# First modulated input of a transformer kernel: built feature-major from a transposed x, its shift and scale as columns

## The chip, the cores and the metric

One core of one Trainium2 chip. The metric is the device time of one execution of the whole program in microseconds; lower is better. Engines are TensorE (PE), VectorE (DVE), ScalarE (ACT), GpSimd (POOL) and SyncE (SP, which here issues all DMAs). Times within the execution are counted from the start of the profiled span.

## What is computed

Two transformer layers (an attention mixer and a gated feed-forward each), then a third block, on a sequence of 256 tokens of 1024 features, in float32. The change touches only how the very first modulated input is made:

```python
shift, scale, gate = split((c @ mod_w[layer, 0] + mod_b[layer, 0])[:, None, :], 3)
h = rms_norm(x, norm_w[layer, 0, 0]) * (1.0 + scale) + shift
y = mixer_ab(h, ...)        # proj = h @ w_in: qa, k, v, gates, qb, kb, vb ...
```

with rms_norm(x, w) = x * rsqrt(mean(x * x) + 1e-6) * w. The vector c has 1024 features; shift and scale are each 1024 wide and the same for all tokens.

## The kernel before

**Products.** A float32 product is made from three products of rounded halves: every weight tile `raw` is split into `whi` (ScalarE, L256) and `wlo` (VectorE, L257), the input into `hhi` and `hlo`, and TensorE makes hhi·whi, hlo·whi and hhi·wlo (L178 to L180). h is held feature-major, as eight k-tiles of 128 features x 256 tokens.

**The start.** `start` makes h in two halves q of four k-tiles (512 features) each. `load(q, v, i)` brings the modulation weights (v = 0 scale, 1 shift) as half-megabyte DMAs and sums over the eight k-tiles kk of c: some kk go to TensorE as a 128x512 product with `cb`, c broadcast to 128 columns (L1550), the others to VectorE, which adds weight times c into `acc` (L1553). `total` adds acc by a product with ones (L1556). All 128 rows of the result are the same, so it stands along the free axis and fits x with tokens on the partitions: `scaled` makes norm weight times (1 + scale) as `ws` (L1566) and multiplies x by it (L1569), `shifted` multiplies by the root and adds the shift (L1575), transposes the eight 128x128 blocks with TensorE (L1578) and evacuates them as hhi (ScalarE, L187) and hlo (VectorE, L188).

**Behind it.** `q_halves` gives the projection qb in two halves of its contraction: `run(0, t)`, t = 0 to 3, uses k-tiles 0 to 3 of h (12 products each) and is called in `start`; `run(1, t)` uses k-tiles 4 to 7 and is called in `mixer_ab`, followed by kb (24 products), the token-major v (L830 to L832), the first scores (L658) and the first softmax (L669). Meanwhile VectorE adds the later modulations in the background (`macc`, L319), the first of them held back until the last hlo of the start.

**What sets the order.** TensorE runs in the order of the program. The order of the other engines' queues, SP's among them, is set by a scheduler when the program is built. Each queue is in order: an instruction that waits holds all behind it. SP's DMAs go round eight semaphores, so that a DMA is issued when the eighth before it has landed; weight tiles go round a ring of six `raw` buffers, splits round four `whi` and four `wlo`. The tiles of `start` share memory with those of the mixer, such as the bias tiles `T` (L844).

In the kernel after, lines up to the start are numbered five higher (L178 is 183, L257 is 262, L319 is 324).

## Time and profile before

| | us |
|---|---|
| median of 3 runs | 1219.04 (1218.2 to 1220.63) |
| the profiled execution | 1217.92 |
| its span | 1216.1 |
| PE busy | 1160.1 (95%) |
| DVE busy | 919.3 (76%) |
| ACT busy | 609.2 (50%) |
| POOL busy | 136.1 (11%) |

The profiled execution is 1.8 us longer than its span, and 1.1 us shorter than the median. Busy shares are averages over stages with different limits; the start, which the change touches, is the first 60 us.

### The profile page before, as it was taken

The numbers are of one execution on the slowest core, as the hardware profiler recorded it, in microseconds if no ns is written. First come the engines' busy times: TensorE is split into PE (matmuls) and PEld (weight loads), VectorE is DVE, ScalarE is ACT, GpSimd is POOL, SyncE is SP. The second block draws the span as 40 slices with busy tenths as digits, with TensorE's granted clock in tenths as the row PEclk, the third lists the DMA queues.
The fourth block names the chain that finished last, engine by engine and source line by source line (L and its number), as shares of the span: only waits on it lengthen the run. The fifth ranks groups of instructions, "written<-read, shape, count | busy, mean of one in ns | idle before, by whom it ended". The sixth has DMA issues, their size and how long they took to land.

```text
span 1216.1 us, 19237 instructions
## 1 busy us (share of the span) xinstructions
PE 1160.1 (95%) x7452; PEld 1010.3 (83%) x7452; DVE 919.3 (76%) x1352; ACT 609.2 (50%) x1107; POOL 136.1 (11%) x181
## 2 busy tenths in 40 slices
PE   6999999999998999999999799999999889999997
PEld 2786569999887965999988699998888657999985
DVE  5888668878759786997896898777569968666545
ACT  2466445444445655554468864544443324445433
POOL 2000010000001012200000200000028850000000
PEclk9999999999999999999999899999999889999999
DMA  9975768868865768777887488688454534665520
GB/s 353 415 263 191 260 242 303 316 219 322 330 221 205 298 217 349 284 293 266 324 314 290 162 299 314 227 300 350 173 195 152 191 139 173 243 234 189 203 103 34
DMA packets 49537, 302.66 MB, mean 249 GB/s; under 512 B 6155, under 2 KB 6283, under 8 KB 16934
## 3 DMA queue, kind: packets, MB, share of 16 engines
q1 hardware_dynamic: 49446, 301.44, 66.7%
q8 instruction: 58, 0.95, 0.3%
q14 instruction: 33, 0.27, 0.1%
HBM read 295.64 MB, written 5.78 MB: 248 GB/s over the span
## 4 chain that ended last, share of the span: by engine, by line
PE 63%; issue 18%; DVE 10%; POOL 3%; ACT 3%; DMA 3%; SPq 0%; POOLq 0%; DVEq 0%; ACTq 0%
PE ps L180 11%; PE ps L178 11%; PE ps L179 11%; PE y L518 5%; PE y L516 5%; PE y L517 5%; PE y L514 4%; PE tok L546 2%; DVE macc L319 2%; DVE wlo L257 1%; PE ps L1305 1%; PE ps L658 1%; DVE st L1357 1%; PE o L702 1%; PE ps L432 1%
## 5 line engine op out<-in xcount | busy, mean ns | idle before, releaser
L256 ACT ACTIVATE whi<-raw 128x1024 fp32r<-128x1024 f32 (+2 forms) x307 | 318.3, 1045 | 374.1 <-PE ps L179 145.6
L257 DVE TENSOR_TENSOR wlo<-raw,whi 128x1024 fp32r<-128x1024 f32 (+2 forms) x307 | 370.3, 1212 | 170.2 <-ACT whi L256 168.5
L180 PE MATMUL ps<-hhi,wlo 128*128 128x256 f32 x1488 | 421.5, 283 | 3.4 <-DVE wlo L257 3.4
L178 PE MATMUL ps<-hhi,whi 128*128 128x256 f32 x1488 | 423.3, 284 | 0.0
L179 PE MATMUL ps<-hlo,whi 128*128 128x256 f32 x1488 | 421.0, 283 | 0.0
L180 PEld LDWEIGHTS ps<-hhi,wlo 128*128 128x128 f32 x1488 | 285.4, 192 | 4.4 <-DVE wlo L257 4.4
L178 PEld LDWEIGHTS ps<-hhi,whi 128*128 128x128 f32 x1488 | 285.3, 192 | 2.3 <-issue 1.1
L179 PEld LDWEIGHTS ps<-hlo,whi 128*128 128x128 f32 x1488 | 285.4, 192 | 1.1 <-DVE wlo L257 0.2
L319 DVE SCALAR_TENSOR_TENSOR macc<-raw,c,macc 128x1024 f32<-128x1024 f32 x152 | 194.9, 1282 | 4.5 <-issue 2.2
L516 PE MATMUL y<-whi,gh 128*128 128x512 f32 x352 | 139.6, 397 | 0.0
L518 PE MATMUL y<-whi,gl 128*128 128x512 f32 x352 | 139.3, 396 | 0.0
L517 PE MATMUL y<-wlo,gh 128*128 128x512 f32 x352 | 139.0, 395 | 0.0
L309 POOL MEMSET macc<- 128x1024 f32 x19 | 18.8, 990 | 582.0 <-DVE mlo L334 556.5
L518 PEld LDWEIGHTS y<-whi,gl 128*128 128x128 f32 x352 | 66.6, 189 | 15.4
L517 PEld LDWEIGHTS y<-wlo,gh 128*128 128x128 f32 x352 | 66.6, 189 | 15.2
L516 PEld LDWEIGHTS y<-whi,gh 128*128 128x128 f32 x352 | 66.6, 189 | 14.9
L514 PE MATMUL y<-raw,o 128*128 128x512 f32 x128 | 57.3, 595 | 0.0
L617 DVE TENSOR_TENSOR g<-sg,ps 128x256 f32<-128x256 f32 x80 | 33.5, 418 | 29.7 <-PE ps L180 29.5
L399 POOL TENSOR_SCALAR ms<-ss 128x1 f32<-128x1 f32 x24 | 11.7, 486 | 377.9 <-ACT junk L409 374.0
L176 PE MATMUL ps<-h,raw 128*128 128x256 f32 x192 | 45.3, 392 | 5.0 <-DVE cvt L1435 5.0
L176 PEld LDWEIGHTS ps<-h,raw 128*128 128x128 f32 x192 | 37.2, 196 | 11.0 <-DVE cvt L1435 5.2
L514 PEld LDWEIGHTS y<-raw,o 128*128 128x128 f32 x128 | 23.5, 190 | 26.3 <-issue 25.1
(313 smaller groups left out, 1458.0 us busy)
## 6 DMA issues: line engine op xcount, KB each, us to landing
raw<-in_mod_dram SPq DMA_DIRECT2D x76, 1024.0 KB
raw<-in_ffn_g_dram SPq DMA_DIRECT2D x44, 1024.0 KB
raw<-in_ffn_u_dram SPq DMA_DIRECT2D x44, 1024.0 KB
raw<-in_ffn_d_dram SPq DMA_DIRECT2D x44, 1024.0 KB
raw<-in_ab_out_dram SPq DMA_DIRECT2D x8, 1024.0 KB
raw<-in_cd_out_dram SPq DMA_DIRECT2D x8, 1024.0 KB
raw<-in_s_c_dram SPq DMA_DIRECT2D x6, 1024.0 KB
raw<-in_s_out_dram SPq DMA_DIRECT2D x6, 1024.0 KB
```

What stands on the lines that cost most here:

```text
L176: mm(out, lh, rh, start=first, stop=last)
L178: mm(out, lh, rh, start=first, stop=False)
L179: mm(out, lh, rl, start=False, stop=False)
L180: mm(out, ll, rh, start=False, stop=last)
L256: self.nc.scalar.activation(hv, src, AF.Copy)
L257: self.nc.vector.tensor_tensor(lv, src, hv.bitcast(F32), ALU.subtract)
L319: nc.vector.scalar_tensor_tensor(acc, box["r"][:, kk % 2], c[:, kk:kk + 1], acc, ALU.mult, ALU.add)
L514: mm(ys[h][b], xh[:, k, c], wh[:, 0, sl], start=first, stop=last)
L516: mm(ys[h][b], xh[:, k, c], wh[:, 0, sl], start=first, stop=False)
L517: mm(ys[h][b], xh[:, k, c], wl[:, 0, sl], start=False, stop=False)
L518: mm(ys[h][b], xl[:, k, c], wh[:, 0, sl], start=False, stop=last)
L617: nc.vector.tensor_tensor(g, sg, pu, ALU.mult)
```

## The change

x comes transposed, as `xt` (eight tiles of 128 features x 256 tokens, 1 MB, in the old place of x in the DMA queue), and norm weight and the two biases as 24 columns `cols`. Scale and shift are wanted as columns, one number per feature on the partitions, so a 128x512 weight block is now the stationary operand, in four blocks of 128 columns, and one column of c is the moving one: four products of 128x1 (changed kernel, line 1554) instead of one of 128x512. `total` does the same with acc and a column of ones (line 1564), and a 128x4 instruction adds the bias and, for the scale, 1 (line 1567). The split of the eight kk between TensorE and VectorE becomes 1, 3, 5, 7 against 0, 2, 4, 6 for the first half and 3, 5, 7 against 0, 1, 2, 4, 6 for the second.

The mean of squares over features is a sum over partitions: ScalarE squares each tile of xt, TensorE adds it by sixteen products with a column of 1/1024 (line 1593). The root stands as a 128x2 tile with tokens on the partitions; the identity times it gives a diagonal, and ones times the diagonal (line 1603) spreads it over all partitions. VectorE multiplies xt by the norm weight and the spread root, in place (line 1605, eight times 128x256). `modulated` makes h from that with scale and shift as columns: t on VectorE (line 1574), hhi on ScalarE, hlo = t - hhi on VectorE (line 1576); nothing is transposed or evacuated. x itself, which the later residual wants, is loaded by a DMA of its own that the scheduler puts behind the last modulation load and ahead of qb's second half, kb and v.

```diff
@@ -128,6 +128,11 @@
     for x, k in enumerate(("ssm_c_re_2", "ssm_c_im_2")):
         ct[:, :, :, x] = I[k][0].reshape(16, 2, 16, 64).transpose(3, 0, 1, 2)[None]
     o["s5_b"], o["s5_cm"] = b.reshape(128, 1024), ct.reshape(128, 1024)
+
+    feat = lambda v: v.reshape(8, 128).T
+    o["xt"] = I["x"][0].T.reshape(8, 128, S).transpose(1, 0, 2)
+    b0 = I["mod_b"].reshape(12, D)
+    o["cols0"] = np.concatenate([feat(I["norm_w"][0, 0, 0]), feat(b0[1]), feat(b0[0])], 1)
     o["mod_bias"] = np.concatenate([I["mod_b"].reshape(12, D), I["b_mod_2"].reshape(9, D)])
     return o
 
@@ -1520,97 +1525,104 @@
         self.c2 = cp.tile([128, 8], F32, name="c2")
         self.x = cp.tile([128, 2, D], F32, name="x")
         with self.tc.tile_pool(name="start", bufs=1) as bp:
-            nw = bp.tile([1, D], F32, name="nw")
             ones = bp.tile([128, 128], F32, name="ones")
             nc.vector.memset(ones, 1.0)
-            cb = bp.tile([128, 8, 128], F32, name="cb")
-            nc.vector.tensor_copy(cb, self.c1.unsqueeze(2).to_broadcast([128, 8, 128]))
+            mean = bp.tile([128, 1], F32, name="mean")
+            nc.vector.memset(mean, 1.0 / D)
+            cols = bp.tile([128, 24], F32, name="cols")
+            xt = bp.tile([128, 8, 256], F32, name="xt")
             hh, hl = self.h = self.h_tiles()
-            rs = []
+            mm = nc.tensor.matmul
 
             def load(q, v, i):
+
 
                 if i == 0:
                     acc = bp.tile([128, 512], F32, name=f"acc{v}{q}")
-                    mods[v] = self.bank([512]), acc, True
+                    sums[v] = [self.bank([4]), acc, True]
                     nc.gpsimd.memset(acc, 0.0)
-                ps, acc = mods[v][:2]
+                ps, acc, _ = sums[v]
                 w = I["mod0"][q, v, i]
                 r = self.raw() if i == 0 and not (q and v) else bp.tile([128, 2048], F32, name="sraw", bufs=5)
                 r = r.rearrange("p (k n) -> p k n", k=4)
-                pairs = [r[:, 0:2], r[:, 2:4]]
                 for k in range(4):
                     kk = 4 * i + k
-                    r = pairs[k // 2][:, k % 2, :]
                     if k % 2 == 0:
-                        nc.sync.dma_start(out=pairs[k // 2], in_=w[:, k:k + 2])
-                        if kk == 0:
-                            nc.sync.dma_start(out=acc[0:1, :], in_=I["mod_bias"][1 - v:2 - v, 512 * q:512 * q + 512])
-                    if kk in (((1, 3, 5, 7), (1, 3, 5, 7)), ((3, 7), (3, 7)))[q][v]:
-                        nc.tensor.matmul(ps, cb[:, kk, :], r, start=mods[v][2], stop=False)
-                        mods[v] = ps, acc, False
+                        nc.sync.dma_start(out=r[:, k:k + 2], in_=w[:, k:k + 2])
+                    if kk in ((1, 3, 5, 7), (3, 5, 7))[q]:
+                        for b in range(4):
+                            mm(ps[:, b:b + 1], r[:, k, 128 * b:128 * b + 128], self.c1[:, kk:kk + 1],
+                               start=sums[v][2], stop=False, skip_group_check=True)
+                            sums[v][2] = False
                     else:
-                        nc.vector.scalar_tensor_tensor(acc, r, self.c1[:, kk:kk + 1], acc, ALU.mult, ALU.add)
-
-            def total(v):
-                nc.tensor.matmul(mods[v][0], ones, mods[v][1], start=False, stop=True)
-                return mods[v][0]
-
-            def scaled(q, ts):
-
-                sl = slice(512 * q, 512 * q + 512)
-                ws = bp.tile([128, 512], F32, name="ws0", bufs=1)
-                nb = self.bank([512])
-                nc.tensor.matmul(nb, ones[0:1, :], nw[:, sl], start=True, stop=True)
-                nc.scalar.activation(ws, nb, AF.Copy)
-                nc.vector.scalar_tensor_tensor(ws, total(0), 1.0, ws, ALU.add, ALU.mult)
-                for h in range(2):
-                    t = bp.tile([128, 512], F32, name="t0", bufs=4)
-                    nc.vector.tensor_tensor(t, self.x[:, h, sl], ws, ALU.mult)
-                    ts.append(t)
-
-            def shifted(q, ts):
-                sh = total(1)
-                for h, t in enumerate(ts):
-                    nc.vector.scalar_tensor_tensor(t, t, rs[h], sh, ALU.mult, ALU.add)
-                    pt = self.bank([4, 128])
-                    for j in range(4):
-                        nc.tensor.transpose(pt[:, j, :], t[:, 128 * j:128 * j + 128], self.ident)
-                    ks, cs = slice(4 * q, 4 * q + 4), slice(128 * h, 128 * h + 128)
-                    self.anchor = self.evac(hh[:, ks, cs], hl[:, ks, cs], pt)
-            mods, ta, tb = {}, [], []
+                        nc.vector.scalar_tensor_tensor(acc, r[:, k], self.c1[:, kk:kk + 1], acc, ALU.mult, ALU.add)
+
+            def total(q, v):
+
+                ps, acc, _ = sums[v]
+                for b in range(4):
+                    mm(ps[:, b:b + 1], acc[:, 128 * b:128 * b + 128], ones[:, 0:1], start=False, stop=b == 3,
+                       skip_group_check=True)
+                m = bp.tile([128, 4], F32, name=f"m{v}{q}")
+                nc.vector.scalar_tensor_tensor(m, ps, 1.0 - v, cols[:, 8 + 8 * v + 4 * q:12 + 8 * v + 4 * q], ALU.add, ALU.add)
+                return m
+
+            def modulated(q, ws, sh):
+                for b in range(4):
+                    k = 4 * q + b
+                    t = bp.tile([128, 256], F32, name="t0", bufs=3)
+                    nc.vector.tensor_scalar(t, xt[:, k], ws[:, b:b + 1], sh[:, b:b + 1], ALU.mult, ALU.add)
+                    nc.scalar.activation(hh[:, k], xt[:, k], AF.Identity, scale=ws[:, b:b + 1], bias=sh[:, b:b + 1])
+                    self.anchor = nc.vector.tensor_tensor(hl[:, k], t, hh[:, k].bitcast(F32), ALU.subtract).ins
+            sums = {}
             load(0, 0, 0)
+            nc.sync.dma_start(out=xt, in_=I["xt"])
             load(0, 0, 1)
-            nc.sync.dma_start(out=self.x, in_=I["x"][0].rearrange("(h p) d -> p h d", p=128))
-            nc.sync.dma_start(out=nw, in_=I["norm_w"][0, 0, 0:1])
-            self.neghalf = cp.tile([128, 4], F32, name="neghalf")
-            nc.vector.memset(self.neghalf, -0.5)
-            for h in range(2):
-                rs.append(self.rstd(*self.mean_sq([self.x[:, h, 512 * q:512 * q + 512] for q in range(2)], D)))
-            scaled(0, ta)
-            load(0, 1, 0)
+            nc.sync.dma_start(out=cols, in_=I["cols0"])
             self.c32 = cp.tile([128, C_W], F32, name="c32")
             nc.sync.dma_start(out=self.c32, in_=I["consts"])
             self.ident = self.c32[:, C_ID:C_ID + 128]
+            self.neghalf = cp.tile([128, 4], F32, name="neghalf")
+            nc.vector.memset(self.neghalf, -0.5)
+
+            ms = self.bank([2])
+            for k in range(8):
+                sq = bp.tile([128, 256], F32, name="sq", bufs=3)
+                nc.scalar.activation(sq, xt[:, k], AF.Square)
+                for h in range(2):
+                    mm(ms[:, h:h + 1], sq[:, 128 * h:128 * h + 128], mean, start=k == 0 and h == 0, stop=k == 7 and h == 1,
+                       skip_group_check=True)
+            ss = self.sp.tile([128, 2], F32, tag="ss", name="ss")
+            nc.vector.tensor_copy(ss, ms)
+            rs = self.rstd(ss)
+            load(0, 1, 0)
+            rb = self.bank([256])
+            for h in range(2):
+                dg = bp.tile([128, 128], F32, name="dg", bufs=2)
+                nc.vector.tensor_scalar(dg, self.ident, rs[:, h:h + 1], None, ALU.mult)
+                mm(rb[:, 128 * h:128 * h + 128], ones, dg, start=True, stop=True)
+            for k in range(8):
+                nc.vector.scalar_tensor_tensor(xt[:, k], xt[:, k], cols[:, k:k + 1], rb, ALU.mult, ALU.mult)
+            ws = total(0, 0)
             load(0, 1, 1)
             nc.sync.dma_start(out=self.c2, in_=I["cond_2"][0].rearrange("(p k) -> p k", p=128))
             nc.scalar.activation(self.c2, self.c2, AF.Silu)
-            shifted(0, ta)
+            modulated(0, ws, total(0, 1))
 
             self.early = prepare, run = self.q_halves(I["ab_qb"], hh, hl)
-            early = {}
             with self.tc.issue_after(self.anchor):
                 early = {t: prepare(0, t) for t in range(4)}
             load(1, 0, 0)
             load(1, 0, 1)
             run(0, 0, early[0])
             run(0, 1, early[1])
-            scaled(1, tb)
+            ws = total(1, 0)
             load(1, 1, 0)
             load(1, 1, 1)
             run(0, 2, early[2])
-            shifted(1, tb)
             run(0, 3, early[3])
+            modulated(1, ws, total(1, 1))
+            nc.sync.dma_start(out=self.x, in_=I["x"][0].rearrange("(h p) d -> p h d", p=128))
 
     def setup(self):
         nc, I, cp, ap = self.nc, self.I, self.cp, self.ap
```

What the scheduler made of it: VectorE's queue, from the spread root to the first splits of qb. acc_201 and acc_255 (before), acc_261 and acc_319 (after) are the second half's scale and shift sums; the hlo here are those of the first half. Before:

```order
L188 TENSOR_TENSOR hlo<-ps,hhi 128x4x128
L1553 SCALAR_TENSOR_TENSOR acc_201<-raw,c_80,acc_201 128x512
L188 TENSOR_TENSOR hlo<-ps,hhi 128x4x128
L257 TENSOR_TENSOR wlo<-raw,whi 128x512 x4
L1553 SCALAR_TENSOR_TENSOR acc_201<-sraw,c_80,acc_201 128x512
L1553 SCALAR_TENSOR_TENSOR acc_255<-sraw,c_80,acc_255 128x512
L1553 SCALAR_TENSOR_TENSOR acc_201<-sraw,c_80,acc_201 128x512
L1553 SCALAR_TENSOR_TENSOR acc_255<-sraw,c_80,acc_255 128x512
L1553 SCALAR_TENSOR_TENSOR acc_201<-sraw,c_80,acc_201 128x512
L1553 SCALAR_TENSOR_TENSOR acc_255<-sraw,c_80,acc_255 128x512 x4
```

After:

```order
L1558 SCALAR_TENSOR_TENSOR acc_319<-sraw,c_80,acc_319 128x512 x2
L1567 SCALAR_TENSOR_TENSOR m_225<-ps,cols 128x4
L1558 SCALAR_TENSOR_TENSOR acc_319<-sraw,c_80,acc_319 128x512
L1574 TENSOR_SCALAR t_227<-xt,m_204,m_225 128x256
L1574 TENSOR_SCALAR t_231<-xt,m_204,m_225 128x256
L1574 TENSOR_SCALAR t_235<-xt,m_204,m_225 128x256
L1558 SCALAR_TENSOR_TENSOR acc_319<-sraw,c_80,acc_319 128x512
L1576 TENSOR_TENSOR hlo<-t_227,hhi 128x256
L1576 TENSOR_TENSOR hlo<-t_231,hhi 128x256
L1576 TENSOR_TENSOR hlo<-t_235,hhi 128x256
L1574 TENSOR_SCALAR t_239<-xt,m_204,m_225 128x256
L1576 TENSOR_TENSOR hlo<-t_239,hhi 128x256
```

All five sums of the second half's shift (one stands two rows above this piece) are now ahead of the first half's first hlo, and the splits of qb follow right behind it; before, nine sums stood behind the hlo and the four splits of qb.

TensorE's queue between the first two and the last two first halves of qb. Before:

```order
L180 MATMUL ps<-hhi,wlo 128x256
L1564 MATMUL ps<-nw,ones 128x512
L1556 MATMUL ps<-acc_201,ones 128x512
L1550 MATMUL ps<-sraw,cb 128x512 x2
L178 MATMUL ps<-hhi,whi 128x256
```

After:

```order
L185 MATMUL ps<-hhi,wlo 128x256
L1564 MATMUL ps<-ones,acc_261 128x1 x4
L1554 MATMUL ps<-c_80,sraw 128x1 x12
L183 MATMUL ps<-hhi,whi 128x256
L184 MATMUL ps<-hlo,whi 128x256
```

The norm weight's product is gone; the total of the scale and the shift's products are four and twelve of one column, where one and two of 512 columns stood.

VectorE's queue around the last hlo and the splits for kb (128x1024) and v (128x816); macc are background sums. Before:

```order
L188 TENSOR_TENSOR hlo<-ps,hhi 128x4x128
L257 TENSOR_TENSOR wlo<-raw,whi 128x512
L257 TENSOR_TENSOR wlo<-raw,whi 128x1024
L257 TENSOR_TENSOR wlo<-raw,whi 128x816 x3
L319 SCALAR_TENSOR_TENSOR macc<-raw,c_80,macc 128x1024 x2
L257 TENSOR_TENSOR wlo<-raw,whi 128x816
```

After:

```order
L1576 TENSOR_TENSOR hlo<-t_389,hhi 128x256
L324 SCALAR_TENSOR_TENSOR macc<-raw,c_80,macc 128x1024
L1632 TENSOR_TENSOR iddup<-c_126 128x128
L324 SCALAR_TENSOR_TENSOR macc<-raw,c_80,macc 128x1024
L262 TENSOR_TENSOR wlo<-raw,whi 128x1024
L324 SCALAR_TENSOR_TENSOR macc<-raw,c_80,macc 128x1024
L262 TENSOR_TENSOR wlo<-raw,whi 128x816
```

Two background sums went ahead of kb's split and a third ahead of v's first.

## Rows read from the trace of the kernel before

**Rows 1.** Table by stage, columns by engine: busy (instructions); PEclk, DMA share, GB/s.

```profile
0.00:5.00 5.00, 0.00 (x0) 0.00 (x0) 1.14 (x4) 1.28 (x1) 3.54 (x9) 1.00 0.46 136
5.00:10.00 5.00, 4.17 (x5) 1.55 (x6) 2.26 (x3) 0.00 (x0) 0.00 (x0) 1.00 1.00 333
10.00:15.00 5.00, 4.34 (x8) 1.40 (x8) 1.10 (x2) 2.00 (x7) 0.49 (x2) 1.00 1.02 413
15.00:20.00 5.00, 4.25 (x10) 1.40 (x9) 4.37 (x7) 2.53 (x5) 3.05 (x3) 1.00 1.03 409
20.00:25.00 5.00, 3.09 (x13) 1.20 (x11) 3.39 (x5) 3.16 (x6) 0.00 (x0) 1.00 1.03 411
25.00:30.00 5.00, 3.58 (x23) 2.86 (x23) 5.00 (x9) 0.00 (x0) 0.00 (x0) 1.00 1.03 412
...
60.00:65.00 5.00, 5.00 (x48) 4.78 (x48) 5.00 (x24) 2.79 (x5) 0.00 (x0) 1.00 1.01 413
65.00:70.00 5.00, 5.00 (x44) 5.00 (x43) 4.97 (x14) 3.45 (x18) 0.00 (x0) 1.00 0.94 324
```

**Rows 2.** Timeline of ScalarE at qb's first split: start, busy, what, idle before.

```profile
21.45 2.19 ACT L256 ACTIVATE whi<-raw 128x512 fp32r<-128x512 f32 x4 [2.16 <-DMA raw<-in_ab_qb_dram]
```

**Rows 3.** Timeline of VectorE, 24 to 51 us.

```profile
24.43 0.68 DVE L188 TENSOR_TENSOR hlo<-ps,hhi 128x512 fp32r<-128x512 f32 x1
...
26.30 2.49 DVE L257 TENSOR_TENSOR wlo<-raw,whi 128x512 fp32r<-128x512 f32 x4
28.70 6.42 DVE L1553 SCALAR_TENSOR_TENSOR acc<-sraw,c,acc 128x512 f32<-128x512 f32 x9
35.04 0.68 DVE L1566 SCALAR_TENSOR_TENSOR ws<-ps,ws 128x512 f32<-128x512 f32 x1
...
41.70 0.68 DVE L188 TENSOR_TENSOR hlo<-ps,hhi 128x512 fp32r<-128x512 f32 x1
...
45.03 2.33 DVE L257 TENSOR_TENSOR wlo<-raw,whi 128x1024 fp32r<-128x1024 f32 x2 [1.32 <-ACT whi L256]
...
50.10 2.60 DVE L319 SCALAR_TENSOR_TENSOR macc<-raw,c,macc 128x1024 f32<-128x1024 f32 x2
```

**Rows 4.** Timeline of TensorE, 5 to 61 us.

```profile
5.28 2.05 PE L1550 MATMUL ps<-raw,cb 128*128 128x512 f32 x2 [5.28 <-DMA raw<-in_mod_dram]
...
15.15 1.88 PE L1550 MATMUL ps<-raw,cb 128*128 128x512 f32 x4
...
27.75 0.28 PE L179 MATMUL ps<-hlo,whi 128*128 128x256 f32 x1
27.86 0.28 PE L180 MATMUL ps<-hhi,wlo 128*128 128x256 f32 x1
27.98 0.28 PE L178 MATMUL ps<-hhi,whi 128*128 128x256 f32 x1
...
51.06 0.35 PE L830 MATMUL tok<-whi,hhi 128*128 128x408 f32 x1
...
60.10 1.16 PE L658 MATMUL ps<-kb,qb 64*128 64x128 f32 x16
```

**Rows 5.** Groups, shapes apart: count, busy us, mean ns, idle; last row: ns min/median/max.

```profile
L1383 DVE SCALAR_TENSOR_TENSOR yg<-u,vec,yp 128x256 f32<-128x256 f32 x4 | 1.9, 468 | 1.2 <-PE yp L176 1.2
...
L968 PE MATMUL ps<-ca,raw 128*128 128x34 f32 x32 | 3.7, 275 | 0.0
...
L643 DVE TENSOR_TENSOR gl<-g,gh x80: 415/418/423, 195.9 to 1148.5; 128x256 fp32r<-128x256 f32 x80
```

**Rows 6.** Table by stage of TensorE: busy (instructions), PEclk, DMA share, GB/s.

```profile
976.00:980.00 4.00, 3.08 (x13) 1.00 0.59 211
980.00:984.00 4.00, 1.09 (x4) 0.61 1.02 432
984.00:988.00 4.00, 4.00 (x10) 0.54 0.35 145
```

**Rows 7.** Chain of waits, the piece at 91 us: start, length, what.

```profile
91.17 1.30 DVE macc L319
```

## The prediction

> **What bounds the kernel now.** I read the start of the span only, since from about 105 us on the two programs hold the same instructions in the same order on every engine; what is lost or gained must arise before that and then be carried to the end, unless something takes it up. The table by stage comes first [rows 1]: from 5 us to 65 us the DMA share is 1.00 or a little more at 410 to 415 GB/s, so in the start a tile lands when the bytes queued ahead of it are through, and no sooner. Adding the rates up to 30 us gives (136 + 333 + 413 + 409 + 411 + 412) x 5 us = 10.57 MB. The sixteen half-megabyte loads of the first modulation, x, the first qb weights and the constants are 10.7 MB, so the last of them is through at about 30.4 us. How much later it can be used is seen at qb: its bytes are through at 20.1 us by the same addition, and ScalarE starts on it at 21.45 [rows 2]. That makes 31.7 us for the last modulation load.
>
> VectorE comes next [rows 3]. In the kernel before, the low halves of the first four k-tiles of h (L188) begin at 24.43, the low halves of qb's weights (L257) at 26.30, and only then the nine sums (L1553) from 28.70. TensorE therefore is at its first three-product work (L178 to L180) at 27.75, while the sums of the second half still arrive [rows 4]. The second half's last low half ends at 41.70 + 0.68 = 42.4 [rows 3]; TensorE reaches the v projection (L830) at 51.06 and the scores (L658) at 60.10 [rows 4]. The start thus has one long chain: last load, sums, h, second halves of qb, kb, v. The end of the kernel moves with it.
>
> **What the change takes away.** The sixteen transposes, the four evacuations and the 128x512 products on the second half's chain: from the ws row to the last hlo row the old chain takes 42.4 - 35.0 = 7.4 us on VectorE's own clock [rows 3]. The new chain after the last sum is four narrow products, a 128x4 instruction, and four tiles of three instructions each. Priced alone that is 0.9 + 0.2 + 4 x 0.35 (t) + 4 x 0.42 (hlo, priced at L643's 128x256 [rows 5]) = 4.2 us, ScalarE's share running beside it. So 3.2 us would be gained, if the chain stood where it stood before. It doesn't.
>
> **What the change moves on VectorE.** In the new queue the first half's t and hlo, and qb's low halves behind them, stand after four of the five sums of the second half's shift (acc_319), and the fifth stands among them, ahead of every hlo. That fifth reads the last modulation load. VectorE's queue is in order, so no hlo can start before 31.7 + 0.7 = 32.4 us, against 24.43: this bound holds whatever the new instructions cost. The work queued puts it later still. From the landing of the second half's first megabyte, about 24.1: one sum to 24.9 (6.42 / 9 = 0.71 each [rows 3]); eight passes xt times weight times root at 0.43 (L1383, 0.47 alone, less the overlap that the sums show, 0.04 [rows 5]), 3.4, to 28.3; six sums, 4.3, to 32.6; two 128x4 instructions, 0.3; three t, 1.0; the fifth sum, 0.7, to 34.6; three hlo, one t, one hlo, 4 x 0.42 less overlap + 0.35 = 1.9, to 36.5 at the latest and, if the t cost as little as 0.25, 36.0. The first low half of qb's weights follows at 0.62 (2.49 / 4 [rows 3]): 36.7. The third product of the first set waits for it. TensorE's dense work thus starts at 36.7, before at 27.5 or so: 9.2 us later.
>
> **What it moves on TensorE.** Its order is the program's. Two first halves, 24 products at 0.12 (27.75, 27.86, 27.98 [rows 4]), 2.9, to 39.6. Then the second half's scale total and its shift products, 4 + 12 narrow ones. A narrow product isn't in the trace; the nearest is L968, 128x34, whose 32 records take 3.7 us or 0.115 each [rows 5]. An fp32 product leaves two records (the row of L1550 at 15.15 holds four for two products [rows 4]), so a narrow product costs 0.23 by this row. Its bounds: 0.115 if one column needs one pass, 0.46 at half clock. I take 0.23: 16 are 3.7, to 43.3. Two more first halves to 46.2, four narrow ones to 47.1. The narrow ones ahead of 31 us cost nothing, as they run between landings. Then m, t, hhi and hlo of the second half: 0.2 + 1.4 + 1.7, to 50.4, where 42.4 stood before. From there the second halves and kb follow as before. Before, 8.7 us lay between the last hlo and L830; the products in it (three runs of 12 and 24 of kb, at 0.12) are 7.2, the rest waits that a later start hides. So L830 comes at 57.6 to 59.1 instead of 51.06, and I take 57.9: **+6.8 us**.
>
> **Steps with a cover.** The 1 MB of x, now issued behind the modulation loads and ahead of qb's second half, puts qb, kb, v and what follows 2.55 us later (1.05 MB at 411 GB/s). All of these land by 40 to 46 us, before TensorE asks for them at 48 to 58; cost 0, and 2.5 if the start ran at its old times. Two background sums (L319) now stand ahead of kb's low half, three ahead of v's first. In the old queue kb's stood at 45.03 and the sums at 50.10 [rows 3]. At 1.3 each they end at 50.4 + 2.6 = 53.0, kb's low half at 54.2, and TensorE comes to kb at about 54.9; the cover is 0.7 us, and without it each sum costs 1.3. The bias tiles T (L844) share their memory with the start's tiles and are issued some 8 us later, with the next query weights behind them on SP; those aren't read before 60 us. The removed bias and norm DMAs are 4 KB at most each: 0.
>
> **TensorE's clock.** The first product of the kernel runs at half speed: two records in 2.05 us, where at 15.15 four take 1.88 [rows 4]; the clock column reads 1.00 there all the same [rows 1], and I go by the durations. From 976 on TensorE is busy 3.08 and then 1.09 of 4 us, and the granted clock falls from 1.00 to 0.61 and 0.54, towards the 1.2 GHz level, where it stays while the next 4 us are full [rows 6]. The new start has only bursts of narrow products until 36.7. I therefore take the clock as half when the dense work starts: the two first halves that come first, 24 products, at 0.24 instead of 0.12, and the rest at the full price: **+2.9 us**.
>
> The Trainium skill, "TensorE: Matmul & The Clock Gate", section "Loop structure matters more than you think", warns of products that each wait for a DMA, since the array then runs at its lower clock. Here the row of 976 to 988 agrees; the 20 to 27 us of the old start, where wide products wait for loads too and the first L179 and L180 still come 0.12 apart [rows 4], speaks against it. By the rule the sum is that with the 2.9, by the old start that without.
>
> **Sum.** 6.8 + 2.9 = 9.7 us on the profiled execution's 1217.9 (span 1216.1 and 1.8 around it): 1227.6. The median of the runs shown is 1.1 above that execution, and a time of the changed kernel may stand as much above this sum, between 1227.6 and 1228.7; I say 1228.
>
> **Rivals.** (a) *The clock is full when the dense work starts.* For it: the old start kept it over half-idle stretches. 1217.9 + 6.8 = 1224.7; with the median 1225.8. With narrow products at 0.115 it would be 1.8 to 2.3 less, at about 1223.
>
> (b) *The narrow products inside the first halves hold the clock down* until the second halves have run for a while. Then the other 24 first-half products cost 2.9 more, the 20 narrow ones 4.6 more, and the start of the second halves 1 to 2 more: 6.8 + 2.9 + 8.5 to 9.5, or 1236 to 1237; with part of it beside VectorE's work, which the late products wait for less then, some 1233.
>
> (c) *The delay is taken up before 105 us.* The order moves three background sums ahead of the first softmax that stood behind it before, 3 x 1.28 = 3.8 us of VectorE; such a sum stands on the chain of waits at 91.17 [rows 7], and the DMA share falls below full from 65 us [rows 1]. If VectorE, not TensorE, sets the stretch from 60 to 105, the 3.8 come back, and with the 3.2 of the shorter h chain the 6.8 are gone: 1217 to 1218, or a little faster. It decides when the sum that stands at 91.17 doesn't move. Against it: that row waits for its loads, which wait for buffers that the late TensorE frees, so they shift too.
>
> (d) *The new h isn't held by the queue*, because the shift's sums are faster than I think. The landing at 31.7 forbids more than 4 us of it; it ends inside (a).
>
> **How the numbers follow.** Forecast 0.38, (a) 0.25, (b) 0.25, (c) 0.12. A measurement of this kernel tells 0.2% (2.4 us) from no change. The first three are all slower by more than that; of (c) 0.05 is faster, 0.06 the same and 0.01 slower. The range has to hold 0.8: from 1222 (the low end of (a), a microsecond under its narrow-product bound) to 1235 (most of (b)); left out are (c) and the end of (b).
>
> **What would show it.** First L180 at 36 to 37; the first hlo right behind the fifth sum of the shift and not before 32.4; the v projection at 57 to 59 at full clock, 60 to 61 at the forecast; the pitch of the first 24 products, 0.24 or 0.12; the shift the same at 105 us and at the end. Wrong it would be if hlo ran before 32, if the macc at 91.17 stood still, or if narrow products took twice 0.23 at full clock.

## The result, and the profile after

| us | median | runs |
|---|---|---|
| kernel before, beside it | 1218.89 | 4 (1218.20 to 1220.63) |
| changed kernel | 1232.23 | 4 (1230.50 to 1233.74) |

The ratio is 1.011, with a 95% interval of 1.0099 to 1.0122: slower by 13.3 us. The profiled execution took 1231.43 us, with a span of 1229.6 against 1216.1. The time lies in the predicted range; the mechanism behind it is in part that of rival (b), not that of the forecast.

The table by stage (stretch, its length, busy time and instructions of PE, PEld, DVE, ACT, POOL, then PEclk, DMA share, GB/s) answers to [rows 1]:

```profile
15.00:20.00 5.00, 5.00 (x25) 5.00 (x25) 2.25 (x3) 3.00 (x6) 0.00 (x0) 1.00 1.03 420
...
35.00:40.00 5.00, 5.00 (x24) 5.00 (x25) 4.00 (x9) 0.03 (x1) 0.00 (x0) 1.00 1.02 411
40.00:45.00 5.00, 5.00 (x40) 5.00 (x39) 1.46 (x3) 1.23 (x2) 0.00 (x0) 1.00 1.02 421
45.00:50.00 5.00, 5.00 (x25) 5.00 (x26) 0.48 (x1) 0.63 (x1) 0.00 (x0) 0.51 0.31 126
50.00:55.00 5.00, 3.65 (x22) 3.37 (x21) 3.10 (x10) 2.71 (x5) 0.00 (x0) 0.80 0.21 52
55.00:60.00 5.00, 4.99 (x29) 4.78 (x28) 5.00 (x7) 2.27 (x4) 0.90 (x4) 0.66 0.93 352
```

TensorE, which before was busy 3 to 4.3 of each 5 us of the start, has no gap from 15 to 50 us; yet with 25 records in 5 us it does no more than one per 0.2 us. The stretch from 45 us has the same 25 records in 5 us and shows why, a granted clock of 0.51, the 1.2 GHz level. Up to some 41.7 us the column reads 1.00 and is wrong, as it was for the first product of the kernel before; the durations tell it. The timeline of TensorE (start, busy, what, idle before) answers to [rows 4]:

```profile
10.71 3.57 PE L1554 MATMUL ps<-c,sraw 128*128 128x1 f32 x16 [1.67 <-DMA sraw<-in_mod_dram]
14.15 6.96 PE L1593 MATMUL ps<-mean,sq 128*128 128x1 f32 x32
...
37.19 0.56 PE L183 MATMUL ps<-hhi,whi 128*128 128x256 f32 x1
37.55 0.41 PE L184 MATMUL ps<-hlo,whi 128*128 128x256 f32 x1
37.76 0.41 PE L185 MATMUL ps<-hhi,wlo 128*128 128x256 f32 x1
...
42.14 0.95 PE L1564 MATMUL ps<-ones,acc 128*128 128x1 f32 x8
42.95 3.27 PE L1554 MATMUL ps<-c,sraw 128*128 128x1 f32 x24
46.08 0.56 PE L183 MATMUL ps<-hhi,whi 128*128 128x256 f32 x1
...
54.33 0.39 PE L184 MATMUL ps<-hlo,whi 128*128 128x256 f32 x1 [0.41 <-DVE hlo L1576]
...
64.72 0.35 PE L835 MATMUL tok<-whi,hhi 128*128 128x408 f32 x1
```

Sixteen records of one-column products last 3.4 us (10.71 to 14.15), 0.21 each, so 0.43 for a product, which leaves two records; at 42.14 eight take 0.81 us, 0.10 each (0.11 in a longer run, below): that is the full clock, and the early ones run at half. The wide products behind them, 0.21 apart at 37.55, are at half too (0.12 before). Between 10.7 and 37.2 stand 120 narrow records and four of L1603, with no wait in between: 120 x 0.213 + 1.1 = 26.7 us, the whole stretch of 26.5. The chain of waits says the same (start, length, what): it runs through TensorE alone.

```profile
2.57 8.10 DMA sraw<-in_mod_dram
10.71 3.57 PE ps L1554 x16
14.29 6.83 PE ps L1593 x32
...
32.21 5.12 PE ps L1554 x24
37.33 0.42 PE ps L183
```

VectorE's timeline, against [rows 3]:

```profile
34.76 1.09 DVE L1576 TENSOR_TENSOR hlo<-t,hhi 128x256 fp32r<-128x256 f32 x3
...
36.62 2.49 DVE L262 TENSOR_TENSOR wlo<-raw,whi 128x512 fp32r<-128x512 f32 x4
...
54.85 0.76 DVE L1576 TENSOR_TENSOR hlo<-t,hhi 128x256 fp32r<-128x256 f32 x2
```

The queue came out much as worked out: the first hlo at 34.76, and qb's first low half, which begins at 36.62, ends at 37.30, 0.6 later than forecast. It is only not what TensorE waits for; no wait stands at 37.19 or at 37.76, though the two lie half a microsecond apart. From the v projection on (64.72 against 51.06, +13.7) the program is shifted nearly as a whole: the scores at 73.76 against 60.10 (+13.7), the first copy of transposed states on ScalarE (sT) at 121.11 against 106.97 (+14.1), the span +13.5.

### The profile page after: what moved, and what is told of

It is laid out like the page before. It is cut to its first block, busy times and chain, and to the rows that moved or that the text cites. A ratio compares the mean times of both kernels' runs of the same rounds, so it can differ in the third digit from the quotient of the medians.

```text
span 1229.6 us, 19499 instructions
## 1 busy us (share of the span) xinstructions
PE 1181.8 (96%) x7580; PEld 1045.2 (85%) x7580; DVE 916.8 (75%) x1367; ACT 611.2 (50%) x1109; POOL 133.6 (11%) x179
## 4 chain that ended last, share of the span: by engine, by line
PE 65%; issue 17%; DVE 9%; POOL 3%; ACT 3%; DMA 2%; SPq 0%; POOLq 0%; DVEq 0%; ACTq 0%
PE ps L183 11%; PE ps L185 11%; PE ps L184 11%; PE y L523 5%; PE y L521 5%; PE y L522 5%; PE y L519 4%; PE tok L551 2%; PE ps L1554 2%; PE ps L663 1%; DVE macc L324 1%; DVE wlo L262 1%; PE ps L1310 1%; PE o L707 1%; DVE st L1362 1%
## 5 line engine op out<-in xcount | busy, mean ns | idle before, releaser
L183 PEld LDWEIGHTS ps<-hhi,whi 128*128 128x128 f32 x1488 | 288.2, 194 | 2.8 <-ACT hhi L1575 1.0
L181 PEld LDWEIGHTS ps<-h,raw 128*128 128x128 f32 x192 | 38.1, 201 | 11.4 <-DVE cvt L1440 5.2
```

Of the source, the lines that this page charges most:

```text
L181: mm(out, lh, rh, start=first, stop=last)
L183: mm(out, lh, rh, start=first, stop=False)
```

## The experiments

Two theories. **A:** TensorE sets the start: 60 of the change's 88 one-column products fill it from 10.7 to 37.2, and at half clock they are themselves the delay; the one-column products also leave the clock at half for what follows. **B:** VectorE's queue sets it, as the prediction had it, and the clock is a detail. The differences below go against the kernel before on the same chip.

**All one-column products made 128 columns wide, every queue's order as in the changed kernel.** The moving operand is the same column 128 times, read with a stride of zero, and only the first result column is used.

```diff
-    sums[v] = [self.bank([4]), acc, True]
+    sums[v] = [self.bank([4, 128]), acc, True]
...
-    ms = self.bank([2])
+    ms = self.bank([2, 128])
...
+    set_columns(nc, 128, lambda i: i.outs[0].ap[1][1] == 1 and len(i.outs[0].ap) == 2)
```

`set_columns` gives the picked products their columns after the queues are in order.

> The changed kernel with every queue in the same order; each of its 88 one-column products moves 128 equal columns instead of one, of which only the first is read. Theory A (the one-column products leave the clock at 1.2 GHz, though TensorE is busy without a gap from 10.7 to 37 us, and let it fall again at 45 us): the products run at the full clock, the first three-product work starts at 36.5 to 37 us and runs at 0.12 us a product, the v projection comes at 57.5 to 59 us instead of 64.7, and the kernel takes 1225 to 1227 us, 6 to 7 less than the changed kernel. Theory B (the queue order and the weight loads of the 88 products, whatever moves through them, make the loss): 1231 to 1234 us, as the changed kernel, or a little more, since 128 columns take no less time than one.

1229.43 (1226.9 to 1232.27), ratio 1.0082 (1.0052 to 1.0112), +10.7 us. TensorE's timeline:

```profile
16.46 1.95 PE L1554 MATMUL ps<-c,raw 128*128 128x128 f32 x16
...
26.75 1.16 PE L1554 MATMUL ps<-c,sraw 128*128 128x128 f32 x8 [0.57 <-DMA sraw<-in_mod_dram]
31.63 0.58 PE L183 MATMUL ps<-hhi,whi 128*128 128x256 f32 x1 [3.73 <-ACT hhi L1575]
33.68 0.58 PE L184 MATMUL ps<-hlo,whi 128*128 128x256 f32 x1 [1.47 <-DVE hlo L1576]
35.81 0.58 PE L185 MATMUL ps<-hhi,wlo 128*128 128x256 f32 x1 [1.54 <-DVE wlo L262]
```

With 128 times the columns the same products take 1.95 us where they took 3.55: the clock is full, and TensorE has waits again. They are through at 27.9, and now VectorE's queue ends last: the third product of the first set comes at 35.81, against 37.76. So A is right on what held TensorE, and the gain is small since B's bound stands 1.9 us behind it. (VectorE's queue is itself earlier here, its first hlo at 33.20 against 34.76: in the changed kernel it had waited for the mean of squares from the slow TensorE.) Behind the waits the clock is at half again (products 0.21 apart from 36.2 to 40.0), so A's forecast of 1225 to 1227 was missed: the time lies between the two theories. The v projection comes 9.0 us late instead of 13.7.

**The other way round: the products stay one column wide, the order is that which the scheduler makes for 128 columns.** In that order the first half's hlo stand ahead of most sums of the second half; the 128-column copy `cb`, one more instruction on VectorE, comes with it.

```diff
-    mean = bp.tile([128, 1], F32, name="mean")
+    mean = bp.tile([128, 128], F32, name="mean")
+    cb = bp.tile([128, 8, 128], F32, name="cb")
...
+    set_columns(nc, 1, lambda i: i.ins[0].memref.startswith(("cb_", "mean_"))
+                or (i.ins[0].memref.startswith("ones_") and i.ins[1].memref.startswith("acc")))
```

> One-column products as in the changed kernel, but the other engines' queues in another order, the one that the scheduler makes when it prices 128 moving columns: the first half's low halves ahead of the second half's sums, kb's and v's low halves ahead of the background sums. Theory A (clock): TensorE is busy with one-column products at half clock until 37 us whatever VectorE does, so the first three-product work still starts at 36 to 37.5 us and the kernel takes 1230 to 1232.5 us, at most 2 less than the changed kernel. Theory B (VectorE's queue sets it): the first three-product work starts at about 28 us and the kernel takes 1219 to 1226 us.

1233.71 (1232.28 to 1235.13), ratio 1.0116 (1.0093 to 1.014), +15.0 us: nothing comes back, and the time is a little above A's forecast.

```profile
37.22 0.56 PE L183 MATMUL ps<-hhi,whi 128*128 128x256 f32 x1
37.58 0.41 PE L184 MATMUL ps<-hlo,whi 128*128 128x256 f32 x1
39.04 0.58 PE L185 MATMUL ps<-hhi,wlo 128*128 128x256 f32 x1 [1.04 <-DVE wlo L262]
```

TensorE reaches its dense work at 37.22, as in the changed kernel at 37.19: the early products at half clock alone forbid an earlier start.

**Both: 128 columns and the order that goes with them.** The same edit without the last line, with `cb` and `ones` read 128 wide.

> Both at once: 128 equal columns moved by each of the 88 products and the scheduler's order for that. If clock and order make the whole loss, the first three-product work starts at 27 to 28 us, the v projection at 51.5 to 53, and the kernel takes 1217 to 1221 us, as the kernel before. If the clock alone counts it stays with the run that only has the 128 columns, 1225 to 1227. If something else of the change costs (the load of x ahead of qb, kb and v, the narrow chain itself), it stays 2 us or more above the kernel before.

1221.97 (1219.05 to 1223.97), ratio 1.002 (1.0008 to 1.0032), +3.3 us.

```profile
27.74 0.36 PE L183 MATMUL ps<-hhi,whi 128*128 128x256 f32 x1
...
31.37 0.58 PE L185 MATMUL ps<-hhi,wlo 128*128 128x256 f32 x1 [3.14 <-DVE wlo L262]
```

The dense work begins at 27.74, half a microsecond later than before the change (27.23); a wait of 3.1 for VectorE is left, with products 0.21 apart behind it until 34. The four corners are +13.3 (neither), +10.7 (columns), +15.0 (order), +3.3 (both). The two delays lie side by side and end within two microseconds of each other, so removing one shows little and removing both gives back 10.

**Only the 20 products in the middle widened** (the second half's scale total, its shift products and the shift's total), then **only the 68 others**. Both keep the order of the changed kernel.

```diff
+    set_columns(nc, 128, lambda i: i.outs[0].memref == "ps_320" or i.ins[1].memref == "acc01_261")
```

> Queues as in the changed kernel; 128 equal columns only in the 20 products that stand between and right behind the first halves of qb, the 68 ahead of these stay one-column. Theory A: the start up to 41.7 us stays as in the changed kernel, at half clock; then the clock stays full, the second 24 products take 2.9 us instead of 5.2 and the second halves run at 0.12; the kernel takes 1226.5 to 1229 us, 3.5 to 6 less than the changed kernel. Theory B: no change, 1231 to 1234 us.

1232.41 (1231.55 to 1233.58), ratio 1.0106 (1.008 to 1.0132). In the profile the clock is full from 43 to 53 us, and the v projection is 11.4 us late instead of 13.7. The 2.3 are given back later, 2.0 of them at a fall of the clock at 169 us that the changed kernel's profile doesn't have; the end is 14.7 late. The second 24 products take 2.9 us, as theory A has it; the time came out as theory B has it. The profile shows one thing more:

```profile
51.24 0.38 PE L183 MATMUL ps<-hhi,whi 128*128 128x256 f32 x1 [1.19 <-ACT hhi L1575]
...
53.03 0.58 PE L184 MATMUL ps<-hlo,whi 128*128 128x256 f32 x1
53.41 0.42 PE L185 MATMUL ps<-hhi,wlo 128*128 128x256 f32 x1
53.63 0.42 PE L183 MATMUL ps<-hhi,whi 128*128 128x256 f32 x1
```

The clock falls a second time, here from 53.0 to 56.4 us, and in the run with all 88 products widened too (50.4 to 53.8), so this fall needs no one-column product ahead of it. It stands behind waits for the second half's h (1.19 and 0.41 us). Whether these make it is open: in the run with both edits the same waits stand at 44 us and the clock stays full.

> The changed kernel with every queue in its order; 128 equal columns only in the 68 products that stand ahead of the first three-product work, the 20 in the middle stay one-column. Theory now: with the clock up, these 68 are done by 28 us, and VectorE's queue (the hlo behind the sums) becomes the bound: the third product of the first set still waits until about 36 us, TensorE waits for it, and the clock falls in that wait. So the loss is hardly smaller than in the changed kernel, 1228 to 1233 us. If the half clock of the first 37 us were a loss by itself, it would be 1226 to 1228.

1231.97 (1228.1 to 1234.42), ratio 1.0107 (1.0084 to 1.013). The early products end at 28.2, but hhi, hlo and wlo are waited for exactly as with all of them widened (the first full set at 36.10), the clock is at half from 32.0 to 52.4 us, and the middle products, narrow again, take 5.26 us where they took 3.27. Neither part alone buys anything.

**Is it the column count, and not the place?** The kernel before, with 24 products of ones by ones, read by nobody, between its second and its third first half; once with one column, once with 128, all queues alike.

```diff
             run(0, 1, early[1])
+            spare = self.bank([4, 128])
+            for i in range(24):
+                nc.tensor.matmul(spare[:, i % 4, 0:1], ones, ones[:, 0:1], start=True, stop=True)
             scaled(1, tb)
```

> The kernel before, with 24 products added that nothing reads: a 128x128 block of ones against one column of ones, put between the second and the third first half of qb, where the clock is full. The start is otherwise the old one. Theory A (one-column products don't hold the clock): the granted clock falls from full to 1.2 GHz within these 24, though TensorE has no gap in them, and the 24 products of the next two first halves run at 0.21 us instead of 0.12; the v projection comes 5 us or more later than in the kernel before (51.06), and the time is 1222 to 1228 us. Theory B (the clock falls only when TensorE waits): the 24 take 24 x 0.21 = 5.1 us at full clock, and what follows runs at 0.12.

> As the run with 24 added one-column products, all queues in the same order, but each moves 128 columns. Theory A: the 24 take 24 x 0.26 = 6.2 us, a little longer than with one column, the clock stays full and the first halves behind them run at 0.12 us a product; the kernel is 1 to 4 us faster than with one column, although the added products take more time. Theory B: no faster, or up to 1 us slower than with one column.

One column: 1227.44 (1224.1 to 1229.95), ratio 1.0078 (1.0059 to 1.0096). 128 columns: 1224.12 (1223.37 to 1225.2), ratio 1.0044 (1.0029 to 1.0059). TensorE's timeline and its table (stretch, length, busy, PEclk, DMA share, GB/s) with one column:

```profile
30.00 5.41 PE L1610 MATMUL ps<-ones 128*128 128x1 f32 x48
35.34 2.01 PE L1564 MATMUL ps<-nw,ones 1*128 1x512 f32 x2
```

```profile
30.00:35.00 5.00, 5.00 (x48) 1.00 1.03 417
35.00:40.00 5.00, 5.00 (x10) 0.54 1.01 409
```

and 128 columns:

```profile
32.30 5.52 PE L1610 MATMUL ps<-ones 128*128 128x128 f32 x48
37.75 1.12 PE L1564 MATMUL ps<-nw,ones 1*128 1x512 f32 x2
```

```profile
35.00:40.00 5.00, 5.00 (x31) 1.00 1.02 408
```

The 48 records take 5.4 and 5.5 us, 0.11 apart in both: 128 columns cost next to nothing more than one, so the moving columns are not the price; what is left in each record is its stationary operand. Both keep TensorE without a gap, and only with the narrow ones does the clock fall to half, at 35.4 us, right behind them, so that the 1x512 products behind take 2.01 instead of 1.12. It fell while TensorE had been busy without a gap from 26.2 us on. (In the second profile the clock had been at half from 24 to 30.7 us, ahead of the added products; it rose there and stayed.) That is A, and 3.3 us between the medians, with intervals that just touch. One detail of the expectation was missed: the first halves behind run at 0.12, since the clock is full again at 42.3; at half run the 512-column products ahead of them.

**x's own load put behind the mixer's first bias tiles.**

```diff
-            nc.sync.dma_start(out=self.x, in_=I["x"][0].rearrange("(h p) d -> p h d", p=128))
+            with self.tc.issue_after(self.bias_dma):
+                nc.sync.dma_start(out=self.x, in_=I["x"][0].rearrange("(h p) d -> p h d", p=128))
```

> The changed kernel with the load of x moved from ahead of qb's second half to behind the bias tiles of the first attention branch, some 25 DMAs later. The prediction put its place at 0 us, as all loads behind it land before TensorE asks for them: 1230.5 to 1233.5 us, as the changed kernel. If the 2.55 us by which it holds up qb, kb and v count: 1228.5 to 1230.

1231.42 (1230.42 to 1233.03), ratio 1.0105 (1.009 to 1.012): 12.3 late against 13.3, whose intervals overlap. The load costs nothing that could be told.

**Versions to beat the kernel before.** All have 128 columns with their order and the late load of x. The first calls `modulated(1, ...)` ahead of the last two first halves; the second also holds most sums of the second half behind the first half's last hlo and gives k-tile 6 of its scale to TensorE; the third holds all those sums and puts the totals behind four first halves.

```diff
+                        with self.tc.issue_after(self.anchor) if q and (v or i) else nullcontext():
+                            nc.vector.scalar_tensor_tensor(acc, r[:, k], self.c1[:, kk:kk + 1], acc, ALU.mult, ALU.add)
...
+            modulated(1, ws, total(1, 1))
             run(0, 2, early[2])
             run(0, 3, early[3])
-            modulated(1, ws, total(1, 1))
```

> The version with 128 columns and its own order, with two edits: the second half's shift total and its h are made ahead of the last two first halves of qb in the program (TensorE waited 1.2 us for them at 43 us), and the load of x goes behind the bias tiles. Theory: the wait for h goes behind 24 products of 0.12, and qb, kb and v land 2.55 us earlier; v projection at 50 to 52 us, 1217 to 1220.5 us, 1.5 to 4 less than the version with 128 columns. If the chain behind the scores (background sums and their loads) is the bound up to 105 us, the gain at the v projection is lost there and the time stays at 1221 to 1223.

> The changed kernel with 128 columns in all its products, the second half's sums on VectorE held behind the first half's last low half, one more k-tile of the second half's scale on TensorE (1, 3, 5, 6, 7), the second half's h ahead of the last two first halves, and x's load behind the bias tiles. Theory: first low half of qb's weights at 29 instead of 36.6 us, TensorE without a wait long enough for the clock to fall, v projection at 49.5 to 51.5, 1215 to 1219 us, at or a little below the kernel before. If the order behind the scores sets the time: 1219 to 1222, as the other versions with 128 columns.

> As the other tuned version, but all of the second half's sums on VectorE are held behind the first half's last low half, and the second half's totals and h stand behind all four first halves in the program. Theory: the first low half of qb's weights a little earlier still (28.8 us), the second half's h no later; v projection at 49.5 to 51.5 us, 1215 to 1219 us.

1220.51 (ratio 1.0016, 1.0005 to 1.0027), 1220.93 (1.0015, 1.0002 to 1.0028) and 1220.33 (1.0019, 1.001 to 1.0028). None beats it. The second is telling: in its profile the v projection comes 1.5 us earlier than before the change, the first sT 5.7 earlier, and at 127 us nothing of it is left. Its chain of waits there:

```profile
106.79 1.20 DVE macc L324
107.98 0.59 DVE p L692 x3
...
109.05 0.58 DVE mlo L339
...
110.94 0.21 DVE pc L1043
111.28 0.66 PE ps L1050 x2
```

and TensorE's table, first of this kernel, then of the kernel before:

```profile
105.00:110.00 5.00, 3.29 (x18) 0.98 0.84 293
110.00:115.00 5.00, 3.87 (x13) 0.50 0.42 177
```

```profile
105.00:110.00 5.00, 2.86 (x13) 1.00 0.99 359
110.00:115.00 5.00, 5.00 (x30) 1.00 0.04 18
```

The earlier start runs into VectorE, which sets the chain from 96 to 111 us with the background sums (`macc`) between the softmax's steps; TensorE waits, and here its clock falls to half on top.

**The 128-column kernel in the changed order once more,** since its first four executions lay from 1226.9 to 1232.3.

> The kernel of cols128 once more, in more executions, to size what TensorE's clock alone costs. Four executions lay in two pairs, near 1227 and near 1232; the profiled one was of the upper pair and ran 100 to 112 us at the half clock. If the pairs are chance of the clock behind the start, executions fall into both groups again, and a profile of the lower group is full at 100 to 112 us, with the v projection about 9 us late and the end 8 to 9 us late. If the widening gives nothing back, the median is within 1.5 us of the changed kernel, 1231 to 1234, and hardly an execution lies at 1227.

1229.88 (1227.43 to 1235.58, 6 executions), ratio 1.0091 (1.0073 to 1.0109). There are no two groups: the ten executions fill the whole stretch. This profile is of the slowest, 1235.58; its start is the same (v projection +9.0), and the table of TensorE shows where the rest comes from:

```profile
95.00:100.00 5.00, 5.00 (x44) 1.00 0.00 1
100.00:105.00 5.00, 5.00 (x26) 0.65 0.48 154
105.00:110.00 5.00, 5.00 (x22) 0.50 0.97 365
...
170.00:175.00 5.00, 4.01 (x6) 0.50 0.58 211
```

The shift of +9.0 becomes +12.5 at 107 and +16.9 at 180 us. Whether an execution near 1227 runs at full clock there stays open, since none of them was profiled.

## Why the prediction was right or wrong

**Range and sign: right.** 1232.2 lies in 1222 to 1235. **The likeliest case: wrong**, by 4 us: 9.7 were forecast, 13.3 came.

**VectorE's queue: right.** No hlo before 32.4 (34.76), the end of qb's first low half at 36.7 (37.30, as 36.62 + 0.68), the third product of the first set at 36 to 37 (37.76 with TensorE late, 35.81 where TensorE is free). The prediction's bound is real, yet it was not the one that ended last. Rival (d) fell with it.

**"The narrow ones ahead of 31 us cost nothing, as they run between landings": wrong.** There was nothing between: at 0.43 each they fill TensorE from 10.7 to 37.2. The prediction had the number, 0.46 at half clock as the upper bound of a narrow product, and weighed it for the 16 in the middle and not for the 60 ahead of them; 60 x 0.46 would have been 27.6 us from the landing at 10.7, beyond 31. It cost only half a microsecond in the sum (37.2 for 36.7), since VectorE's queue lay beside it. That the two bounds lie so close is luck; the step hid the second one. The price at full clock, 0.23 forecast, was 0.22 (two records 0.11 apart).

**The clock's term: mis-sized, and this is the miss.** The clock was at half when the dense work started, as forecast, though not behind bursts with gaps: TensorE had no gap ahead of it. The prediction put 24 products at half and "the rest at the full price", 2.9 us. The first 24 went from 37.33 to 42.30, where 36.7 to 42.5 was worked out: they began 0.6 later and took 5.0 instead of 5.8 us, since the clock rose within them, and the two misses offset each other. The 16 narrow ones behind them ended at 46.1, by the same sum at 46.2. Then the step fails. The clock, full from 41.8, was at half again at 46.08, behind these 16 narrow ones: the next 24 products took 46.08 to 51.35, 5.3 instead of 2.9 us, **+2.4**. It was at half once more from 55.33 to 58.67, 15 products at 0.21 or a little more instead of 0.12, **+1.5**. Together 3.9, and the v projection came at 64.7 where the forecast has 57.9 + 2.9 = 60.8. The profile with the middle products widened confirms the first: full clock there, and the v projection 2.3 earlier. The second stands in that profile too, so it doesn't need the narrow products; its cause stays open.

**Rival (b)** named the first of these two ("hold the clock down until the second halves have run for a while") and priced the whole at 1233 to 1237. With 1232.2 it came out just under its low end, since the narrow products in the middle ran mostly at full clock: 32 records from 42.14 to 46.08, 0.12 each, 0.3 us more than their forecast price, where (b) gave the 20 narrow ones 4.6. It had 1 to 2 us for the start of the second halves as well, and 1.5 came there; but the same fall comes with the narrow products widened, so this agreement is luck.

**On the rule of the Trainium skill** weighed in the prediction, "TensorE: Matmul & The Clock Gate", which in its section "HAM oscillation — how this bites in real kernels" speaks of idle gaps of TensorE: by that rule alone a TensorE without a gap from 10.7 on would have been taken at the full clock. This case shows a fall without any gap, 0.54 right behind 48 back-to-back records of one column, against 1.00 with 128. The Trainium skill, on the same page, section "LDWEIGHTS (loading the stationary operand)", gives a weight load a time by its columns, an estimate of 128 / 1.2 = 107 ns for 128 of them; the trace agrees at the full clock, with 0.11 us per one-column record, and at half clock, where the record took 0.21, it doesn't.

**Rival (c): wrong,** as argued against it. The sum that stood at 91.17 [rows 7] did not stand still: the corresponding sum begins at 103.83.

```profile
103.83 2.61 DVE L324 SCALAR_TENSOR_TENSOR macc<-raw,c,macc 128x1024 f32<-128x1024 f32 x2 [2.53 <-DMA macc<-in_mod_bias_dram]
```

**Steps with a cover: right.** x's load cost nothing that could be told; kb's low half ran at 58.12, and TensorE did not wait for it. **Rival (a),** the full clock when the dense work starts, didn't come up; the 128-column kernel in the same order shows that even with full-clock products ahead the first sets run at half, behind the waits for hhi, hlo and wlo.

## What to carry to other kernels

Turning a product round so that the wide operand is stationary and one column moves saved nothing on TensorE here: four products of one column are 0.9 us at the full clock, and the 128x512 product that they replace takes as long (four records in 1.88 us [rows 4]). A run of such products, though TensorE is never idle, can leave the clock at half for itself and for the dense work behind. Where the result is wanted as a column, pad the moving side to 128 columns: 48 records took 5.5 us so, and 5.4 with one column. That made up most of the loss here, together with the order of VectorE's queue; it did not make the change a gain. And when a new operation is given a price with bounds, carry the upper bound through every place where the operation stands, those that seem free too: the delay that ends second shows itself only when the first is removed.

## What the runs showed of the hardware

A busy share of 1.00 did not keep the clock up, which had not been expected. In the four profiles whose early products move one column TensorE has no gap from 10.7 to 37 us and stays at half until 41.7 to 44.1 us; in the seven in which these products move 128 columns the clock is first full at 8.7 to 16.8 us. The pair of 24 added products shows the same for a fall, with the same queues.

The other falls remain unexplained. The kernel has 32 records of 34 columns back to back (L968 before, L973 after), between 85 and 108 us in the fourteen profiles. In nine of them the clock falls to half within these records or right behind them, in the changed kernel at 106.6 us (0.66 from 105 to 110); in the other five, that of the kernel before among them, it doesn't. So the fall changes from one profile to the next, which fits the spread of 4 to 8 us between executions of one kernel; that these records are its cause was seen beside the falls, not tested.
